# Prompt's pointwise jobs put ahead of four output units, partial sums added in DRAM, and the sample's last scaling spread out on GpSimd's queue

## The chip, the core and the metric

The kernel runs on one core of a Trainium2 chip. The metric is device microseconds of one execution, from the host's side; lower is better. TensorE (PE) does the matmuls, VectorE (DVE), ScalarE (ACT) and GpSimd (POOL) the rest, and SyncE (SP) issues most of the transfers between DRAM and SBUF. GpSimd issues the transfers that add into their target. In the listings of this text, `out<-in` names what an instruction writes and reads, and a number behind a name is a buffer's.

## What is computed

One encoder layer over two sequences with shared weights: the *sample* (1024 positions) and the *prompt* (512), both with 2048 channels in fp32.

```python
def mixer_layer(x, norm_g, w_in, w_dw, b_dw, ln_g, ln_b, w_pw, sink, w_out):
    h = rms_norm(x, norm_g)
    z = h @ w_in                       # conv value, glu, gate; q, k, v; attention gate
    ...
    conv_out = conformer_conv(c_val, c_glu, w_dw, b_dw, ln_g, ln_b, w_pw) * silu(c_gate)
    attn_out = banded_sink_attention(q, k, v, sink) * silu(a_gate)
    mix = concatenate([conv_out, attn_out], axis=-1) @ w_out
    return x + mix

y = rms_norm(mixer_layer(x, ...), final_norm_g)     # for x_prompt and x_sample
```

Inside `conformer_conv` a layer norm and a silu stand ahead of the *pointwise* product with `w_pw` (1024 x 1024). The case here lies in the last steps of both sequences: the prompt's pointwise product, its product with `w_out`, the sum with x and the last norm; and for the sample only the last norm's scaling.

## The kernel before

Every fp32 product is made of three matmuls on parts of reduced precision: a value is split into a high part (a copy on ACT, line 449) and a low part (a subtraction on DVE, line 450), and high x high, high x low and low x high are summed in a PSUM bank. On top of this the large products use a Strassen-like scheme: a *unit* takes a 2 x 2 arrangement of weight blocks and token blocks and forms seven products P1, P2, P6, P5, P7, P3, P4 of sums and differences of blocks. So weights need subtractions on DVE (line 138, `sub`) before they are split, and so do tokens.

The end of the program runs in this order. `over[1]` are eight units of the sample's out-projection, the last of which is called `end`; each finished piece goes to `y_d` in DRAM and its squares are summed (`Mix.project`). Then come four *wide* units for the prompt's out-projection (class `Wide`), each with p, the half of the output's columns, and g, the half of the input channels: g = 1 is the attention's half, g = 0 the convolution's. A wide unit has seven steps of 24 matmuls of 128x512 and loads fourteen tiles of 512 KB, eight of `w_last` (weights in rows) and six of `low_out` (low parts stored earlier by the sample's units). Between the second and the third wide unit stand the prompt's eight pointwise *jobs* `fj`, of 24 matmuls each, since the g = 0 units need their result as tokens.

The parts that the change touches:

- **The prompt's partial sums.** In a g = 1 unit, `Wide.tap` (line 1678) takes a finished bank out with ACT or DVE, adds banks of the same output block on DVE (line 1693, 1699) and stores four sums for each of two row blocks into `part_d` (called `rows` in listings), in pieces of 512 bytes. Before the g = 0 units, `load_rows` (line 1515) loads rows of x into SBUF by SP and then adds `part_d` to them by a transfer of GpSimd (line 429, `add_into`). In g = 0 units `add_rows` (line 1532) adds each bank to these rows on DVE (line 1536), and after the last one takes squares, multiplies by the gain, scales and stores.
- **The sample's last scaling.** `Mix.finish` (line 1280) waits until all squares are there, makes the factors, and then, for each of 16 channel blocks, loads 512 KB of `y_d`, multiplies on DVE (line 1311) and stores to `y_s`, all by SP. It is a generator on the lane `prep`, which advances by a credit of nanoseconds for each matmul group that is written out; `yield 2500` is the price of one block.
- **Buffers.** T1 (28 tiles of 4 KB per partition) holds tokens and wide weights, F (7), A (4), G (4) and U (4) hold rows and intermediate results. `E()` takes from G and U in turn. `raw` (3) and `hl` (3) hold weights ahead of and behind the split. A load into a buffer waits until the last reader of what was in it is done.

Engines run their instructions in the order of the listing. A scheduler that knows dependences and priorities makes that order from the program, so an instruction without dependences may be listed far ahead of where the code asks for it. A wait holds up all that stands behind it on the same engine or queue.

Of the kernel before, what the change touches and what calls it, by code (L numbers as in the profile page):

```python
# [7 lines left out]
F32 = mybir.dt.float32  # L8
# [1144 lines left out]
class Mix:  # L1153


    def __init__(self, e, seq, out):
# [8 lines left out]
        self.squared = 0  # L1165
        self.beside = []
# [113 lines left out]
    def finish(self):  # L1280
# [28 lines left out]
        for o in range(ND):  # L1309
            y = held.popleft()  # L1310
            nc.vector.scalar_tensor_tensor(y, y, e.fin_g[:, o : o + 1], rb, ALU.mult, ALU.mult)
            e.store(self.out[o], y)
            y = None
            load(o + 2)
            yield 2500
# [126 lines left out]
class LastPost(Post):  # L1442


    def __init__(self, e, seq, t0, out, mix):
# [3 lines left out]
        self.x, self.s1 = [], {}  # L1449
        self.part_d = [[e.tc.dram_tile([P, NB, 2, P], F32, name=f"rows_{b}{c}") for c in range(2)] for b in range(NB)]  # L1450
# [15 lines left out]
    def load_attention(self):  # L1466
        e = self.e
        for h in range(0, HEADS, 2):
            t = (e.F if h < HALF else e.A)([2, W], F32)
            e.nc.sync.dma_start(t, self.seq.att_d[h // GROUP][:, h % GROUP : h % GROUP + 2, :])  # L1470
            self.x.append(t)

    def load_gate(self, i):
# [3 lines left out]
        if i % 2 == 0:  # L1477
            t = e.A([2, W], F32)
            self.x.append(t)
# [4 lines left out]
    def mixed(self, i, f):  # L1484
        if i % 2:
            n = i // 2 % 2
            self.token(0, "A11" if i < HALF else "A12", n)
            if i == HALF + 1:
                self.token(0, "S2", n)

    def token(self, g, name, n):
# [3 lines left out]
        x0 = half(self.x[n])  # L1495
        x1 = half(self.x[n + 2]) if name != "A11" else None
# [11 lines left out]
        if name == "A22" and n == 1:  # L1508
            self.x = []
# [4 lines left out]

    def load_rows(self, c, room):
        e, half = self.e, D // 2
        for b in range(NB):
            t = self.rows[b][c] = room([half], F32)
            e.nc.sync.dma_start(t, self.e.a["x_p"][b * P : (b + 1) * P, c * half : (c + 1) * half])
        for b in range(NB):  # L1520
            e.add_into(self.rows[b][c], self.part_d[b][c].rearrange("p a c x -> p (a c x)"))

    def load_gain(self):
        e, half = self.e, D // 2
        for c in range(2):
            self.gain[c] = e.F([half])
# [36 lines left out]
class Wide(Unit):  # L1563


    def __init__(self, e, last, p, g, tags):
# [4 lines left out]
        self.raw, self.low, self.sum, self.d = {}, {}, {}, {}  # L1571
# [107 lines left out]
    def tap(self, name, q):  # L1679

        e, nc, d = self.e, self.e.nc, self.d
# [9 lines left out]
        if name in ("P2", "P3"):  # L1691
            x = d.pop((q, c))
            nc.vector.tensor_tensor(x, bank, x, ALU.add)
        else:
            x = e.PT("p", NP, [W]) if name == "P6" else e.E()
            nc.scalar.activation(x, bank, AF.Copy)
            if name == "P7":
                y = d.pop((q, 2))
                nc.vector.tensor_tensor(x, x, y, ALU.add)
            elif name != "P4":  # L1700
                d[q, {"P1": 0, "P6": 1, "P5": 2}[name]] = x
        if last:
            e.store_later(self.last.part_d[b][self.p][:, :, c, :], x.rearrange("p (a x) -> p a x", a=NB))


def encoder(ctx, tc, a):
# [234 lines left out]
    def norm_last():  # L1941
# [9 lines left out]
        Wide(e, last, 0, 1, ("ss", "bc", "aa")),  # L1951
        Wide(e, last, 1, 1, (("pt", "pv"), "bc", "aa")),
        Wide(e, last, 0, 0, (("pt", "pv"), "bc", "aa")),
        Wide(e, last, 1, 0, ("ss", "bc", "aa")),
# [8 lines left out]
    end.before.append(last.load_attention)  # L1963
    for step, name in enumerate(names):
        at(end, step, lambda name=name: e.T.pop(name))
    for unit, step, name in ((end, 0, 0), (end, 2, 1), (end, 4, 2), (wide[0], 0, 3), (wide[0], 1, 4), (wide[0], 2, 5), (wide[0], 3, 6)):
        at(unit, step, lambda name=names[name]: last.tokens(1, name))
    for step, name in enumerate(names):
        at(wide[1], step, lambda name=name: last.tok[1].pop(name))
        at(wide[3], step, lambda name=name: last.tok[0].pop(name))  # L1970
    wide[1].before.append(lambda: e.prep.add(mix.finish()))
    pace(wide[1], 1.5, e.prep)
    for step in (2, 4):
        for i in range(4):
# [67 lines left out]
```

## Time and profile before

| | us |
|---|---|
| three runs, median (lowest to highest) | 2160.98 (2159.86 to 2161.76) |
| the profiled execution | 2158.56 |
| its span in the trace | 2156.8 |
| TensorE busy | 2072.4 (96% of the span) |
| DVE, ACT, POOL busy | 1750.3, 1133.6, 111.8 |
| bytes moved by DMA | 498.72 MB, mean 231 GB/s |

The span is the trace's own length, from the first to the last instruction; the 1.8 us between it and the execution's time lie around it. "L1311" is line 1311 of the program. A row of waits names who waited for what. TensorE's busy time counts modelled ends of pipelined matmuls, so the idle time is better read from stretches than from the sum. SP's and POOL's transfers run on queues that the profile calls q1 (SP) and q0 (POOL).

### The profile page before, as it was taken

The page shows a single profiled execution, that of the slowest core. Times are in us where ns is not written, and L with a number is a line of the kernel's source. Part 1 is how long each engine was busy: PE and PEld are TensorE (multiplying, and loading weights), DVE is VectorE, ACT ScalarE, POOL GpSimd, SP SyncE. Part 2 cuts the span into 40 slices and gives each one's busy share as a digit, 9 for nine tenths or more (in the row PEclk, how much of TensorE's full clock was granted, in tenths as well). Part 3 has the DMA queues.
Part 4 walks back from the last instruction along what each step waited for, and adds up shares of the span by engine and source line. Part 5 has one row for each costly group of instructions (what it writes and reads, how often), then busy time and mean ns, then how long its engine had stood idle before and what let it go on. Part 6 is the DMA issues. An engine that isn't in the chain of part 4 may idle for free.

```text
span 2156.8 us, 26835 instructions
## 1 busy us (share of the span) xinstructions
PE 2072.4 (96%) x9234; PEld 1695.2 (79%) x9234; DVE 1750.3 (81%) x2655; ACT 1133.6 (53%) x1832; POOL 111.8 (5%) x132
## 2 busy tenths in 40 slices
PE   8999999999999999999999999999999999979857
PEld 7878888888888887788888888878878888758646
DVE  8657798988898988988987786578997779687747
ACT  7475445333555556555556764245644645555324
POOL 0001110000011111000000000000000011100000
PEclk9999999999999999999999999999999999989979
DMA  8888888854777778654465548977896699987884
GB/s 298 291 287 242 227 185 265 284 175 144 245 180 181 167 161 268 209 176 152 150 211 181 183 135 293 324 251 260 283 301 215 198 296 267 281 298 250 337 248 152
DMA packets 246713, 498.72 MB, mean 231 GB/s; under 512 B 22704, under 2 KB 84528, under 8 KB 246576
## 3 DMA queue, kind: packets, MB, share of 16 engines
q1 hardware_dynamic: 227136, 458.72, 63.3%
q0 software_dynamic: 18432, 35.66, 10.2%
q10 hardware_dynamic: 1008, 2.63, 0.3%
q8 instruction: 72, 1.18, 0.2%
q14 instruction: 65, 0.53, 0.1%
HBM read 335.97 MB, written 160.96 MB: 230 GB/s over the span
## 4 chain that ended last, share of the span: by engine, by line
PE 79%; DMA 10%; DVE 5%; issue 3%; ACT 2%; POOL 0%; SPq 0%; POOLq 0%; ACTq 0%; DVEq 0%
PE a L191 23%; PE a L588 12%; PE c L191 11%; PE c L588 6%; PE b L191 6%; PE b L588 5%; PE s L191 3%; PE s L1052 2%; PE pv L1084 2%; PE a L1641 2%; PE s L1641 2%; DVE hl L450 1%; DMA f<-x_s 1%; PE pt L1089 1%; DMA f<-rows 1%
## 5 line engine op out<-in xcount | busy, mean ns | idle before, releaser
L191 PE MATMUL a<-t,hl 128*128 128x512 f32 x2640 | 633.4, 390 | 6.7 <-ACT u L217 4.2
L191 PEld LDWEIGHTS a<-t,hl 128*128 128x128 f32 x2640 | 493.5, 188 | 113.3 <-ACT u L217 6.7
L925 DVE SCALAR_TENSOR_TENSOR f<-f,c_w_dw,f 128x1024 f32<-128x1024 f32 (+1 forms) x464 | 455.9, 1015 | 0.9 <-ACT f L920 0.8
L450 DVE TENSOR_TENSOR hl<-raw,hl 128x1024 fp32r<-128x1024 f32 (+1 forms) x304 | 306.8, 1009 | 155.9 <-ACT hl L449 154.9
L449 ACT ACTIVATE hl<-raw 128x1024 fp32r<-128x1024 f32 (+1 forms) x304 | 268.9, 885 | 300.6 <-DVE raw L138 59.4
L588 PE MATMUL a<-t,hl 128*128 128x512 f32 x1344 | 328.5, 394 | 1.1 <-DVE hl L450 1.1
L191 PE MATMUL c<-t,hl 128*128 128x512 f32 x1320 | 319.5, 390 | 1.7 <-ACT u L217 0.9
L191 PEld LDWEIGHTS c<-t,hl 128*128 128x128 f32 x1320 | 247.5, 188 | 54.6 <-ACT g L217 1.7
L588 PEld LDWEIGHTS a<-t,hl 128*128 128x128 f32 x1344 | 248.6, 188 | 52.2 <-DVE hl L450 2.2
L588 PE MATMUL c<-t,hl 128*128 128x512 f32 x672 | 166.1, 394 | 0.9 <-DVE hl L450 0.6
L588 PE MATMUL b<-t,hl 128*128 128x512 f32 x672 | 164.0, 393 | 0.7 <-DVE hl L450 0.7
L191 PE MATMUL b<-t,hl 128*128 128x512 f32 x660 | 161.6, 390 | 0.0
L588 PEld LDWEIGHTS b<-t,hl 128*128 128x128 f32 x672 | 124.6, 188 | 26.1 <-DVE hl L450 1.1
L588 PEld LDWEIGHTS c<-t,hl 128*128 128x128 f32 x672 | 124.1, 188 | 26.0 <-DVE hl L450 1.0
L191 PEld LDWEIGHTS b<-t,hl 128*128 128x128 f32 x660 | 123.4, 188 | 25.2
L217 ACT ACTIVATE u<-a 128x512 f32<-128x512 f32 x114 | 67.4, 592 | 86.5 <-PE a L191 64.6
L217 ACT ACTIVATE g<-a 128x512 f32<-128x512 f32 x106 | 62.8, 592 | 76.2 <-PE a L191 68.2
L1641 PE MATMUL a<-hl,t 128*128 128x512 f32 x160 | 50.4, 439 | 28.4 <-DVE f L1536 14.2
L1066 ACT ACTIVATE p<-p,tiny 128x384 f32<-128x384 f32 (+1 forms) x96 | 54.5, 570 | 30.1 <-DVE tiny L1063 18.8
L449 ACT ACTIVATE a<-pt 128x512 fp32r<-128x512 f32 x64 | 38.0, 594 | 51.9 <-PE pt L1089 51.7
L346 ACT ACTIVATE hl<-raw 128x1024 fp32r<-128x1024 f32 x44 | 46.3, 1052 | 35.6 <-PE a L588 12.4
L1641 PEld LDWEIGHTS a<-hl,t 128*128 128x128 f32 x160 | 33.2, 212 | 39.2 <-issue 14.3
(354 smaller groups left out, 2690.7 us busy)
## 6 DMA issues: line engine op xcount, KB each, us to landing
raw<-w_in SPq DMA_DIRECT2D x171, 512.0 KB, 4.8
t<-w_last SPq DMA_DIRECT2D x32, 512.0 KB, 7.8
raw<-w_out SPq DMA_DIRECT2D x31, 512.0 KB, 5.4
a<-xT_s SPq DMA_DIRECT2D x50, 256.0 KB, 5.4
raw<-w_pw SPq DMA_DIRECT2D x24, 512.0 KB, 5.1
t<-low_out SPq DMA_DIRECT2D x24, 512.0 KB, 8.1
f<-x_s SPq DMA_DIRECT2D x16, 512.0 KB, 7.2
low_out<-hl SPq DMA_DIRECT2D x16, 512.0 KB, 4.2
```

The lines of the kernel that those rows point to most:

```text
L191: nc.tensor.matmul(acc, hl[:, l, o, j, :], toks[j][:, r], start=name in FRESH and j == 0 and q == 0, stop=name in LAST and j == HALF - 1 a ...
L217: nc.scalar.activation(t, bank, AF.Copy)
L346: e.nc.scalar.activation(t[:, 0], raw, AF.Copy)
L449: nc.scalar.activation(hi, x, AF.Copy)
L450: nc.vector.tensor_tensor(lo, x, hi.bitcast(F32), ALU.subtract)
L588: nc.tensor.matmul(job.acc[0], hl[:, l, kk // HALF, kk % HALF, :], r, start=i == 0 and p == 0, stop=i == nk - 1 and p == 2,)
L925: nc.vector.scalar_tensor_tensor(t, h[:, j : j + T], w(j), t, ALU.mult, ALU.add)
L1052: nc.tensor.matmul(ps[:, 0:n], qs[:, x, h], k[y][:, keys], start=p == 0, stop=p == 2)
L1066: nc.scalar.activation(p[:, 0:n], p[:, 0:n], AF.Exp, bias=nm[:, h : h + 1], accum_out=l[:, h : h + 1])
L1084: nc.tensor.matmul(pv, v[x][:, vs], pt[:, y], start=i == 0 and p == 0, stop=i == last and p == 2)
L1089: nc.tensor.transpose(tp[:, h], p[:, i * P : (i + 1) * P], e.ident)
L1641: nc.tensor.matmul(self.bank[n][q], tok[h][:, r, i, q * P : (q + 1) * P], e.hl[at[h]][l][:, i], start=name in FRESH and j == 0 and p == 0, ...
```

## The change

The eight pointwise jobs now stand ahead of all four wide units. The sums of the g = 1 units are no longer formed in SBUF: x is copied to `part_d` ahead of time, each bank is copied out by ACT and added into `part_d` by a transfer of GpSimd, and the rows are then loaded whole. The sample's scaling takes a price of 8000 in place of 2500 for each block, and its loads and stores go in halves through GpSimd's queue. The gain is loaded into raw buffers in place of F buffers. The prompt's tokens are made by `tokens` alone, in steps of the wide units, and the units' PSUM banks are dealt anew.

```diff
 # Mix.finish
-                nc.sync.dma_start(held[-1], self.y_d[o])
+                for t in (0, W):
+                    nc.gpsimd.dma_start(held[-1][:, t : t + W], self.y_d[o][:, t : t + W])
...
+        self.spread = True
...
-            e.store(self.out[o], y)
+            for t in (0, W):
+                nc.gpsimd.dma_start(self.out[o][:, t : t + W], y[:, t : t + W])
             y = None
             load(o + 2)
-            yield 2500
+            yield 8000
 # LastPost
-        self.part_d = [[e.tc.dram_tile([P, NB, 2, P], F32, ...
+        self.part_d = [[e.tc.dram_tile([P, 2, W], F32, ...
...
+    def copy_row(self, b, c):
+        e, half = self.e, D // 2
+        src = e.a["x_p"][b * P : (b + 1) * P, c * half : (c + 1) * half]
+        for i in range(2):
+            dst = self.part_d[b][c][:, i].rearrange("p (a x) -> p a x", a=NB)
+            e.nc.sync.dma_start(dst, src.rearrange("p (a c x) -> p a c x", a=NB, c=2)[:, :, i])

     def load_rows(self, c, room):
         for b in range(NB):
             t = self.rows[b][c] = room([half], F32)
-            e.nc.sync.dma_start(t, self.e.a["x_p"][b * P : (b + 1) * P, c * half : (c + 1) * half])
-        for b in range(NB):
-            e.add_into(self.rows[b][c], self.part_d[b][c].rearrange("p a c x -> p (a c x)"))
+            for i in range(2):
+                e.nc.sync.dma_start(self.columns(t, i), self.part_d[b][c][:, i].rearrange("p (a x) -> p a x", a=NB))

     def load_gain(self):
-            self.gain[c] = e.F([half])
+            self.gain[c] = e.raw_tile().rearrange("p a b c -> p (a b c)")
 # Wide.tap, g == 1
-        if name in ("P2", "P3"):
-            x = d.pop((q, c))
-            nc.vector.tensor_tensor(x, bank, x, ALU.add)
-        else:
-            x = e.PT("p", NP, [W]) if name == "P6" else e.E()
-            nc.scalar.activation(x, bank, AF.Copy)
...
-        if last:
-            e.store_later(self.last.part_d[b][self.p][:, :, c, :], x.rearrange("p (a x) -> p a x", a=NB))
+        x = e.E()
+        nc.scalar.activation(x, bank, AF.Copy)
+        e.add_into(self.last.part_d[b][self.p][:, c], x)
 # encoder
+    for n, unit in enumerate(over[1]):
+        at(unit, 3, lambda n=n: last.copy_row(n // 2, n % 2))
...
-    fj[3].before.append(lambda: last.load_rows(0, e.F))
-    fj[7].before.append(last.load_gain)
...
+    fj[1].before.append(lambda: e.prep.add(mix.finish()))
+    pace(fj[1], 1.5, e.prep)
...
+    wide[1].before.append(lambda: until(lambda: mix.spread, e.prep))
+    at(wide[1], 2, last.load_gain)
+    at(wide[1], 4, lambda: last.load_rows(0, e.F))
+    at(wide[2], 3, lambda: last.load_rows(1, e.A))
+    at(wide[3], 3, e.prep.drain)
...
-    jobs += [[wide[0]], [wide[1]]] + [[j] for j in fj] + [[wide[2]], [wide[3]]]
+    jobs += [[j] for j in fj] + [[w] for w in wide]
```

Three places in the listings show what moves. The first is SP's queue ahead of the third wide unit, before the change: the loads of x (L1519) stand behind the stores of the sample's rows and between the unit's weights, and GpSimd's adds wait for them.

```order
L432 DMA y_s<-f_2541_17003 128x1024
L432 DMA y_s<-f_2542_17013 128x1024
L432 DMA y_s<-f_2547_17035 128x1024
L1519 DMA f_2550_17068<-x_p 128x1024
L1519 DMA f_2551_17070<-x_p 128x1024
L1593 DMA t1_2619_17473<-w_last 128x1024
L1598 DMA t1_2620_17475<-low_out_10_414 128x1024
```

After the change the same queue, at the end of the pointwise jobs' loads: the last job's weights, two loads of the gain, and then the loads of the first wide unit.

```order
L332 DMA raw_2420_16404<-w_pw 128x1024
L1485 DMA a_2438_16505<-gate_d1_7_168 128x512
L1532 DMA raw_2551_17114<-final_gain 128x1024
L1532 DMA raw_2552_17116<-final_gain 128x1024
L1598 DMA t1_2445_16529<-w_last 128x1024
L1603 DMA t1_2446_16531<-low_out_00_412 128x1024
L1598 DMA t1_2449_16561<-w_last 128x1024
L1603 DMA t1_2450_16563<-low_out_00_412 128x1024
```

The sample's rows and x are gone from here; the weights follow one another. The second place is the wide units. GpSimd's queue after the change, from the first step of the first wide unit on: `rows` are the adds of banks (L429), `y_s` and `y_d` the sample's stores and loads (L1316, L1289).

```order
L429 DMA rows_10_266<-g_2472_16666 128x512
L1316 DMA y_s<-f_2463_16620 128x512 x2
L429 DMA rows_00_264<-u_2480_16717 128x512
L429 DMA rows_10_266<-g_2481_16720 128x512
L1289 DMA f_2466_16646<-y_d_2_206 128x512 x2
L429 DMA rows_00_264<-u_2491_16775 128x512
L429 DMA rows_10_266<-g_2492_16778 128x512
L1316 DMA y_s<-f_2464_16623 128x512 x2
L1289 DMA f_2477_16702<-y_d_3_207 128x512 x2
```

Before, this queue held eight adds into rows behind the last out-projection unit's and nothing else; now adds, stores and loads take turns in it. DVE in the second wide unit after the change: L1314 is the sample's scaling, L450 a low part of weights (`hl`) or tokens (`t1`).

```order
L450 TENSOR_TENSOR hl_2557_17129<-t1_2519_16931,hl_2557_17129 128x1024
L1314 SCALAR_TENSOR_TENSOR f_2531_17007<-f_2531_17007,c_final_norm_g_957,f_2220_15033 128x1024
L450 TENSOR_TENSOR hl_2559_17151<-t1_2522_16949,hl_2559_17151 128x1024
L450 TENSOR_TENSOR t1_2561_17168<-a_2391_16219,t1_2561_17168 128x512
L450 TENSOR_TENSOR t1_2563_17175<-a_2399_16291,t1_2563_17175 128x512
L1314 SCALAR_TENSOR_TENSOR f_2546_17078<-f_2546_17078,c_final_norm_g_957,f_2220_15033 128x1024
```

Before, most of these scalings stood among the pointwise jobs, and four of them in a row ahead of the third unit's tokens. The third place is SP's queue near the program's start, as one piece of the difference: the copies of x to `rows` (L1519), which the code asks for in `over[1]`, are listed among the first stage's stores and loads.

```order
 L432 DMA part_conv_01_293<-u_909 128x512
+L1519 DMA rows_264<-x_p 128x4x128
 L432 DMA part_conv_10_288<-g_1011 128x512
+L1519 DMA rows_264<-x_p 128x4x128
+L1519 DMA rows_265<-x_p 128x4x128
 L432 DMA part_conv_10_294<-u_1038 128x512
+L1519 DMA rows_265<-x_p 128x4x128
+L1519 DMA rows_266<-x_p 128x4x128
 L123 DMA raw_1044<-w_in 128x1024
```

Six of the sixteen copies stand here; the other ten follow within a hundred rows.

More of the change, by code (lines that the diff above doesn't have):

```diff
@@ L1448, in __init__ @@
         self.tok = {0: {}, 1: {}}
[L1449 to L1450 removed]
+        self.x, self.s1 = {0: [], 1: []}, {}
+        self.part_d = [[e.tc.dram_tile([P, 2, W], F32, name=f"rows_{b}{c}") for c in range(2)] for b in range(NB)]
         self.rows = [[None, None] for _ in range(NB)]
@@ L1570, in __init__ @@
         self.order = ALONE
-        self.raw, self.low, self.sum, self.d = {}, {}, {}, {}
+        self.raw, self.low, self.sum = {}, {}, {}
     LOADS = {"P1": [(0, 0)], "P2": [(0, 1)], "P6": [(1, 0), (1, 1)]}
@@ L1950, in encoder @@
     wide = [
[L1951 to L1954, printed above, removed]
+        Wide(e, last, p, g, banks)
+        for p, g, banks in (
+            (0, 1, (("pt", "pv"), "bc", "aa")),
+            (1, 1, ("ss", "bc", "aa")),
+            (0, 0, (("pt", "pv"), "bc", "aa")),
+            (1, 0, ("ss", "bc", "aa")),
+        )
     ]
@@ L1962, in encoder @@
     end = over[1][-1]
-    end.before.append(last.load_attention)
     for step, name in enumerate(names):
         at(end, step, lambda name=name: e.T.pop(name))
-    for unit, step, name in ((end, 0, 0), (end, 2, 1), (end, 4, 2), (wide[0], 0, 3), (wide[0], 1, 4), (wide[0], 2, 5), (wide[0], 3, 6)):
-        at(unit, step, lambda name=names[name]: last.tokens(1, name))
-    for step, name in enumerate(names):
         at(wide[1], step, lambda name=name: last.tok[1].pop(name))
         at(wide[3], step, lambda name=name: last.tok[0].pop(name))
[L1971 to L1974, printed above, removed]
-            at(wide[1], step, lambda i=i, step=step: last.split(2 * step - 4 + i))
+    for step in range(2):
+        for i in range(4 * step, 4 * step + 4):
+            at(end, step, lambda i=i: last.split(i))
+    at(end, 2, last.load_attention)
+    for n, unit in enumerate(over[1]):
+        at(unit, 3, lambda n=n: last.copy_row(n // 2, n % 2))
     def run_out():
@@ L1979, in run_out @@
             e.turn_over(True)
-    fj[3].before.append(run_out)
-    fj[3].before.append(lambda: last.load_rows(0, e.F))
-    fj[7].before.append(e.prep.drain)
-    fj[7].before.append(last.load_gain)
-    for step, name in ((0, 2), (0, 3), (1, 4), (2, 5), (3, 6)):
-        at(wide[2], step, lambda name=names[name]: last.tokens(0, name))
-    at(wide[2], 0, last.cs.clear)
-    at(wide[2], 4, lambda: last.load_rows(1, e.A))
-    jobs += [[wide[0]], [wide[1]]] + [[j] for j in fj] + [[wide[2]], [wide[3]]]
+    fj[5].before.append(run_out)
+    fj[1].before.append(lambda: e.prep.add(mix.finish()))
+    pace(fj[1], 1.5, e.prep)
+    for n, name in ((2, 0), (4, 1), (6, 2)):
+        fj[n].before.append(lambda name=names[name]: last.tokens(1, name))
+    for step, name in enumerate(names[3:]):
+        at(wide[0], step, lambda name=name: last.tokens(1, name))
+    at(wide[0], 0, last.cs.clear)
+    for step, name in enumerate(names):
+        unit, n = (wide[1], step + 1) if step < 5 else (wide[2], step - 5)
+        at(unit, n, lambda name=name: last.tokens(0, name))
+    wide[1].before.append(lambda: until(lambda: mix.spread, e.prep))
[4 more added lines that the diff above has]
+    jobs += [[j] for j in fj] + [[w] for w in wide]
     e.weights_setup(jobs)
```

25 lines of the change are left out of this document (8 added, 17 removed).

## The prediction

> **What bounds the kernel now.** I first cut the end of the run into its stages with the view that sums busy time by stretch. The columns are the stretch and its length, then the busy time of PE, PEld, DVE, ACT and POOL, the granted TensorE clock (1.00 is full), the mean busy share of the 16 DMA engines, and GB/s.
>
> ```profile
> 1700.00:1883.00 183.00, 180.55 (x797) 147.02 (x796) 146.13 (x226) 106.74 (x178) 27.03 (x31) 1.00 0.94 276
> 1883.00:1941.00 58.00, 44.25 (x168) 33.88 (x167) 45.25 (x57) 29.19 (x41) 0.86 (x1) 0.85 0.88 298
> 1941.00:1982.00 41.00, 41.00 (x190) 33.95 (x189) 33.08 (x65) 26.78 (x37) 0.00 (x0) 1.00 0.67 217
> 1982.00:2026.00 44.00, 44.00 (x196) 36.45 (x195) 28.64 (x31) 11.77 (x14) 0.00 (x0) 1.00 0.97 353
> 2026.00:2105.00 79.00, 46.52 (x169) 34.72 (x168) 46.90 (x56) 24.16 (x36) 4.56 (x6) 0.78 0.82 269
> 2105.00:2143.50 38.50, 38.50 (x171) 31.64 (x169) 33.11 (x58) 19.87 (x32) 2.40 (x3) 1.00 0.34 85
> 2143.50:2156.80 13.30, 0.12 (x1) 0.00 (x0) 6.08 (x22) 4.46 (x9) 0.00 (x0) 0.68 0.80 316
> ```
>
> The rows are: the last out-projection units, the first wide unit, the second, the eight pointwise jobs, the third wide unit, the fourth, the tail. TensorE is full in all but the first and third wide units. All four units have the same matmuls, and the fourth shows what one costs when it is served: 38.5 us. The second takes 41.0 with extra small matmuls for the sample's norm. So the four parts between 1883 and 2105 need 44.0 + 41.0 + 2 x 38.5 = 162 us of TensorE and take 222: **60 us are lost**, 19.5 in the first unit and 40.5 in the third, part of it to a clock that is not granted in full (0.85 and 0.78). This is all that the end of the kernel can give. Next, the waits, first TensorE's own from 1883 to 2106, then the longest of DVE in 2026 to 2106 (total, times, longest).
>
> ```profile
> PE a L1641 <- DVE f L1536: 14.2, 2, 13.9
> PE a L1641 <- DVE t L450: 9.4, 2, 7.1
> PE s L1641 <- ACT hl L449: 8.5, 1, 8.5
> PE pt L1641 <- DVE f L1536: 6.4, 2, 5.6
> ...
> DVE f L1536 <- DMA f<-rows: 22.5, 4, 10.7
> ```
>
> In the third unit TensorE waits for a free bank, the bank for DVE's add into the rows (L1536), and DVE for the rows, which came by two transfers in series (x, then an accumulating one). In the first unit the waits (ACT hl L449, DVE t L450) are for weights and tokens that are late. Last, the queues and issues from 1883 to 2105 (packets, MB, share of 16 engines; KB each, us to landing).
>
> ```profile
> q1 hardware_dynamic: 24900, 59.40, 75.3%
> q0 software_dynamic: 1152, 3.41, 8.3%
> ...
> t<-w_last SPq DMA_DIRECT2D x28, 512.0 KB, 7.5
> t<-low_out SPq DMA_DIRECT2D x19, 512.0 KB, 7.6
> f<-y_d SPq DMA_DIRECT2D x16, 512.0 KB, 6.5
> y_s<-f SPq DMA_DIRECT2D x16, 512.0 KB, 6.3
> ...
> f<-x_p SPq DMA_DIRECT2D x4, 512.0 KB, 6.1
> f<-rows POOLq DMA_DIRECT2D x4, 512.0 KB, 11.1
> a<-x_p SPq DMA_DIRECT2D x4, 512.0 KB, 7.2
> rows<-g SPq DMA_DIRECT2D x6, 256.0 KB, 3.8
> rows<-u SPq DMA_DIRECT2D x6, 256.0 KB, 3.8
> rows<-p SPq DMA_DIRECT2D x4, 256.0 KB, 3.1
> ```
>
> So beside TensorE stands a second resource that is nearly full: 83.6% of 222 us, 186 us of all 16 engines. TensorE needs 162 us, the transfers 186. The 60 us are waits in series today, but 24 us of them remain even if every wait goes, unless bytes go or move.
>
> **The change part by part.** *Order of stages.* The pointwise jobs come directly behind the out-projection. They need weights through the raw buffers, and eight split tiles made in the last out-projection unit, so the first unit's late weights no longer face an idle TensorE: the listing has one unit's loads issued under the jobs. Two gain loads stand ahead of twelve of these on SP's queue and wait for raw buffers, until about the fourth job (22 us in); 22 us are left for 14 x 0.52 = 7.3 MB, which at the 353 GB/s of the jobs' row take 21. I cost this at nothing; without that cover it would be a few us at the first unit's start. The splits (8 on ACT, 8 on DVE) move into a stretch where DVE is busy 146 of 183 us and ACT 107, so they fit.
>
> *Rows.* The third unit's serial wait (x_p, then 11.1 us) goes, since the loads are issued in the second unit. What is late next is the DMA engines. Prices: on q1, 0.753 x 222 = 167 us for 59.40 MB, 2.81 us per MB. An accumulating transfer, from the window, 0.083 x 222 / 3.41 = 5.4 us per MB; over the whole run:
>
> ```profile
> q0 software_dynamic: 18432, 35.66, 10.2%
> ```
>
> 0.102 x 2156.8 / 35.66 = 6.2, twice the price of a plain one (191 ns of an engine per packet against 96 if q1's price is put on the same 2 KB). Plain bytes of the same stretch afterwards: 59.4, less x_p (8 x 0.52 = 4.2), less the stores to rows (16 x 0.26 = 4.2), plus 16 row loads of 0.26 (4.2): **55.2 MB, 155 us**. Accumulating: 14 adds per unit and two units, 28 x 0.26 = 7.3 MB, and one old one: 7.6 MB at 5.4 to 6.2, **44 us**. Together **199 us**, where there were 186. The work on DVE shrinks by 12 adds and ACT's grows by 8 copies of some 0.6 us, both beside TensorE.
>
> The change thus takes away waits and adds 13 us to the resource that is nearly full. If the engines run unbroken, the stretch takes 199 us instead of 222: TensorE loses 37 instead of 60, **a gain of 23 us**. The place is the second and third unit's weights and the sample's rows. The fourth unit and the tail (38.5 and 13.3) stay.
>
> The bounds of the prices. The best stretch of the page's kind:
>
> ```profile
> 2020.00:2040.00 20.00, 17.18 (x76) 13.89 (x74) 16.60 (x20) 9.14 (x12) 0.00 (x0) 1.00 1.01 405
> ```
>
> At 405 GB/s a MB costs 2.5 us: 55.2 MB take 138, with the adds at 5.4 (41) 179, lost 17, gain 43. If the engines hold only the 0.94 of the first row above, 199 / 0.94 = 212, lost 50, gain 10. No run shows an add whose target is DRAM; the rows above have SBUF as target. Below, it could cost as little as a plain one (2.8 us per MB: 23 us less); less than plain is excluded, since it moves the same bytes. Above, I allow twice the seen price (12.4 at most: some 45 us more). I take the seen price, the nearest row.
>
> The Trainium skill, "DMA: Bandwidth & Descriptors", section on issuing engines that are not separate DMA queues, says that transfers issued by GpSimd, SP or ACT run on the same 16 engines, and that another issuer saves only issue time. It speaks against the move of the sample's 16.8 MB to GpSimd's queue; by it the sum is the 199 us above. Were it wrong, SP's queue would keep 38.4 MB, 108 us, below TensorE's 162, and nearly all 60 us would come back. No row before the change tries it, but no stretch here shows a share much over 1.
>
> *The sample's scaling.* Per row it is one DVE operation:
>
> ```profile
> L1311 DVE SCALAR_TENSOR_TENSOR f<-f,c_final_norm_g,f 128x1024 f32<-128x1024 f32 x16 | 20.0, 1279 | 2.0 <-DMA f<-y_d 2.0
> ...
> L429 POOL DMA_DIRECT2D g<-part_out x16 | 14.5, 907 | 67.0 <-DVE g L237 39.8 <-ACT g L217 11.3 <-DMA f<-att_d 7.4
> ```
>
> The listing has sixteen such operations strewn from the first unit's start to the third's middle, one every 6 us. Halves make 64 issues on POOL beside 28 adds: 92 x 0.9 = 83 us of POOL in 162, which fits. What is new is the wait: behind each scaling on DVE stand the next low parts of weights and tokens, and the row it waits for is issued on POOL behind adds that wait for ACT's copies, and behind the store that frees its buffer.
>
> *Copies of x.* The code asks for them in the out-projection; the listing puts all 16 (4.2 MB, 12 us at 2.81) among the first loads.
>
> ```profile
> 40.00:170.00 130.00, 126.79 (x553) 102.85 (x552) 86.98 (x144) 80.50 (x134) 0.00 (x0) 1.00 0.87 295
> ```
>
> There 13% of 130 us, 17 us, are free, so most is hidden; bounds 0 and 12 us, and I take **2 us**.
>
> **Sum.** The profiled execution took 2158.56 us, 2.4 below the median of the runs shown. 2158.6 - 23 + 2 = 2137.6; on the median's scale **2140**.
>
> **The rivals.** *Hidden after all:* adds in DRAM cost what plain transfers do, or the engines run at the best stretch's rate. Gain 35 to 60, so 2103 to 2128. For it: rates of 405 exist. Against it: mixed stretches run at 250 to 350.
>
> *GpSimd's queue in series:* while only two buffers turn over, a row needs a store (two issues of 0.9, landing 6.3), a load (1.8 and 6.5) and the scaling (1.3): 17.7 us for two rows, 8.8 each, against 5.5 us for a step of TensorE (38.5 / 7). Some five rows are held so, 5 x 3.3 = 17 us if that time doesn't fall on the engines' own excess: 2157. For it: the listing's order. Against: four more buffers come free in the first unit.
>
> *Slower, by the price of an add in DRAM:* 28 adds are 224 packets of 2 KB on each engine, so each ns more per packet adds 0.224 us. The net gain of 21 us is gone when a packet costs 94 ns more than 191, from about **285 ns**; at twice the price, 382 ns, the result is 2161 - 21 + 43 = 2183. For it: the sum already exceeds TensorE's work, so every added us shows. Against: adds from DRAM into SBUF cost just two plain packets.
>
> **How the numbers follow.** The forecast (gain 10 to 34, 2129 to 2153) has 0.45, the hidden case 0.18, the queue in series 0.17 (2150 to 2160, about 0.05 of it clear of no change), the dear adds 0.20 (2163 to 2185). The forecast's own range is 2129 to 2153; for 8 in 10 it must reach into both outer cases: 2112 to 2172. About 0.2%, 4.3 us, is what a measurement of this kernel can tell from no change. Faster 0.45 + 0.18 + 0.05 = 0.68, within 0.12, slower 0.20.
>
> **What would show it.** Right: behind the out-projection the jobs run full; DVE no longer waits for rows; the three wide units after them take about 155 us at a DMA share of 0.95 or more; TensorE waits there for low parts of weights that stand behind the scaling on DVE. q0 carries some 56 MB (35.7, less 4.2 for the rows' old adds, plus 7.3 and 16.8), and its adds cost near 191 ns per packet. The first 170 us stay as full as they are. Wrong: a DMA share well under 0.9 in the wide units with TensorE waiting (series on a queue), TensorE full there (hidden), or a long row of waits for ACT's copies to find a free buffer (dear adds).

## The result, and the profile after

| | before | after |
|---|---|---|
| median of 4 runs (lowest to highest), us | 2161.02 (2159.86 to 2161.76) | 2146.86 (2142.96 to 2149.76) |
| the profiled execution, its span | 2158.56, 2156.8 | 2147.58, 2145.8 |

The ratio is 0.9934, interval 0.9917 to 0.9951: faster by 14.2 us, where 21 were forecast, inside the range. First the view that sums busy time by stretch, cut at the ends of the stages after the change: the eight pointwise jobs, the four wide units, the tail. The columns are those of the prediction's first view.

```profile
1888.60:1934.50 45.90, 45.90 (x212) 38.21 (x211) 26.96 (x62) 14.39 (x19) 1.75 (x2) 1.00 0.89 319
1934.50:1989.60 55.10, 43.20 (x170) 33.47 (x169) 36.75 (x41) 27.73 (x39) 21.16 (x31) 0.88 0.91 267
1989.60:2040.20 50.60, 43.37 (x170) 34.10 (x169) 35.26 (x38) 28.35 (x41) 22.73 (x36) 0.90 1.04 332
2040.20:2094.10 53.90, 40.70 (x170) 32.62 (x169) 35.52 (x42) 19.79 (x30) 14.07 (x22) 0.87 1.01 318
2094.10:2132.00 37.90, 37.90 (x168) 31.00 (x167) 34.58 (x60) 19.23 (x33) 0.00 (x0) 1.00 0.14 44
2132.00:2145.80 13.80, 1.06 (x5) 0.56 (x3) 6.87 (x24) 5.39 (x9) 0.00 (x0) 0.69 0.77 304
```

The jobs are full, and so is the fourth unit (37.9). The first three units, at 55.1, 50.6 and 53.9, lose 45.9 us against it, where the stretch of before lost 60. The DMA engines stand at 0.91 to 1.04 in them, and at 0.14 in the fourth. From the jobs' start to the third unit's end it takes 205.3 us, before 221.8. The queues in just that stretch (packets, MB, share of 16 engines):

```profile
q1 hardware_dynamic: 17894, 38.67, 52.1%
q0 software_dynamic: 9440, 24.40, 44.0%
```

That is 96.1% of 205.3 us, or 197 us of all engines, where 199 were forecast. So the transfers cost what was worked out; the stretch is longer than they are. What TensorE waits for from 1875 us on (total, times, longest):

```profile
PE a L1646 <- DVE hl L450: 11.8, 1, 11.8
PE pt L1646 <- DVE hl L450: 8.5, 2, 7.6
PE s L1646 <- DVE hl L450: 7.2, 3, 4.3
PE pt L1646 <- ACT hl L449: 2.7, 1, 2.7
```

And DVE, in the wide units:

```profile
DVE f L1314 <- DMA f<-y_d: 50.7, 8, 11.6
```

The old waits for the prompt's rows (DVE f L1536, 22.5 us) are gone. In their place 27.5 of 32.4 us of TensorE's waits are for low parts of weights (`hl`, L450), and DVE, which makes them, stands 50.7 us ahead of the sample's scaling (L1314) until its row has come. The rest of the 45.9 us is clock. In the timeline of TensorE's matmuls (start, us, what, how many, idle before):

```profile
1974.88 0.50 PE L1646 MATMUL pt<-hl,t 128*128 128x512 f32 x1 [0.91 <-DVE t L450]
1982.94 0.79 PE L1646 MATMUL pt<-hl,t 128*128 128x512 f32 x1 [7.56 <-DVE hl L450]
1983.53 1.48 PE L1646 MATMUL pv<-hl,t 128*128 128x512 f32 x3
1984.81 1.48 PE L1646 MATMUL pt<-hl,t 128*128 128x512 f32 x3
...
1987.96 0.85 PE L1646 MATMUL pv<-hl,t 128*128 128x512 f32 x3
1988.65 0.85 PE L1646 MATMUL pt<-hl,t 128*128 128x512 f32 x3
```

Behind a wait of 7.56 us three matmuls take 1.28 us from one start to the next (1983.53 to 1984.81), and some 4 us later 0.69 (1987.96 to 1988.65). So a wait costs more than its own length: 32.4 us of waits, and some 13 more at a granted clock of 0.87 to 0.90. The Trainium skill, "TensorE: Matmul & The Clock Gate", Part 1, says that the clock falls to half after an idle window of about 3.4 us and comes back after as long a busy one; these rows agree, with slow matmuls for some 4 us behind a wait of 7.56.

### The profile page after: what moved, and what is told of

Read it like the earlier page. It is cut to its first block, busy times and chain, and to the rows that moved or that the text cites. A ratio compares the mean times of both kernels' runs of the same rounds, so it can differ in the third digit from the quotient of the medians.

```text
span 2145.8 us, 26961 instructions
## 1 busy us (share of the span) xinstructions
PE 2073.5 (97%) x9234; PEld 1698.2 (79%) x9234; DVE 1740.5 (81%) x2643; ACT 1136.5 (53%) x1840; POOL 165.2 (8%) x216
## 3 DMA queue, kind: packets, MB, share of 16 engines
q0 software_dynamic: 26432, 55.59, 13.2%
## 4 chain that ended last, share of the span: by engine, by line
PE 76%; DMA 9%; DVE 7%; issue 4%; ACT 2%; POOL 1%; SPq 1%; ACTq 0%; POOLq 0%; DVEq 0%
PE a L191 23%; PE a L588 12%; PE c L191 11%; PE b L588 6%; PE c L588 6%; PE b L191 6%; PE s L1052 2%; PE pv L1084 2%; DMA f<-y_d 2%; PE s L191 2%; DVE hl L450 2%; PE pt L1089 1%; PE s L1646 1%; DMA f<-x_s 1%; DVE f L925 1%
## 5 line engine op out<-in xcount | busy, mean ns | idle before, releaser
L450 DVE TENSOR_TENSOR hl<-raw,hl 128x1024 fp32r<-128x1024 f32 (+1 forms) x304 | 305.7, 1005 | 156.6 <-ACT hl L449 155.5
L588 PEld LDWEIGHTS b<-t,hl 128*128 128x128 f32 x672 | 124.5, 188 | 26.1 <-DVE hl L450 1.1
L429 POOL DMA_DIRECT2D u<-part_out x16 | 14.0, 893 | 933.4 <-DMA f<-msum_S 875.7
L1066 ACT ACTIVATE p<-p,tiny 128x384 f32<-128x384 f32 (+1 forms) x96 | 54.5, 570 | 32.3 <-DVE tiny L1063 21.1
L449 ACT ACTIVATE t<-f 128x512 fp32r<-128x512 f32 x87 | 50.4, 622 | 31.8 <-DMA f<-cs 13.3
L449 ACT ACTIVATE a<-pt 128x512 fp32r<-128x512 f32 x64 | 38.0, 593 | 52.2 <-PE pt L1089 52.0
```

What stands on the lines that cost most here:

```text
L449: nc.scalar.activation(hi, x, AF.Copy)
L450: nc.vector.tensor_tensor(lo, x, hi.bitcast(F32), ALU.subtract)
L588: nc.tensor.matmul(job.acc[0], hl[:, l, kk // HALF, kk % HALF, :], r, start=i == 0 and p == 0, stop=i == nk - 1 and p == 2,)
L1066: nc.scalar.activation(p[:, 0:n], p[:, 0:n], AF.Exp, bias=nm[:, h : h + 1], accum_out=l[:, h : h + 1])
```

## The experiments

Two theories were set against each other. *A, engine time:* the prediction's, that the transfers' time on the 16 engines sets the length of the wide units. *B, order:* the sample's rows are late because their loads and stores take turns with the adds in GpSimd's queue, and DVE waits for them ahead of the low parts. Each ratio is to the kernel before, timed beside the run. The lengths of the four units are worked out from the start times of the matmuls in the profiled execution (168 per unit, from the back; the last column is their sum), good to about half a microsecond. `price14000` and `no_finish` leave out part of the sample's scaling, and `plain_stores` the sums.

| run | median, us | ratio to before (interval) | wide units 1, 2, 3, 4 | sum |
|---|---|---|---|---|
| the change | 2146.9 | 0.9934 (0.9917 to 0.9951) | 55.1, 50.6, 53.9, 38.2 | 197.8 |
| `after_again` | 2146.9 | 0.9937 (0.9922 to 0.9951) | 54.9, 51.3, 52.6, 38.1 | 196.9 |
| `plain_stores` | 2124.9 | 0.9839 (0.9823 to 0.9855) | 51.8, 38.1, 50.8, 37.9 | 178.6 |
| `sp_finish` | 2146.7 | 0.9936 (0.9920 to 0.9953) | 44.1, 50.7, 63.4, 37.8 | 196.0 |
| `price14000` | 2135.2 | 0.9885 (0.9871 to 0.9900) | 44.2, 40.9, 59.2, 40.0 | 184.3 |
| `price13000` | 2137.0 | 0.9905 (0.9883 to 0.9927) | 44.1, 42.9, 60.5, 37.9 | 185.4 |
| `sbuf_sums` | 2141.4 | 0.9925 (0.9906 to 0.9945) | 54.5, 41.0, 58.7, 40.5 | 194.7 |
| `sums_spread11` | 2137.4 | 0.9909 (0.9888 to 0.9931) | 46.2, 41.7, 55.8, 40.9 | 184.6 |
| `order_only` | 2148.0 | 0.9933 (0.9918 to 0.9948) | 48.2, 57.7, 54.4, 37.9 | 198.2 |
| `rows_late` | 2146.2 | 0.9924 (0.9909 to 0.9939) | 54.4, 51.0, 53.4, 38.1 | 196.9 |
| `rows_sums_spread` | 2138.3 | 0.9889 (0.9873 to 0.9906) | 46.9, 40.1, 59.0, 40.5 | 186.5 |
| `no_finish` | 2119.2 | 0.9808 (0.9788 to 0.9827) | 44.1, 38.7, 52.2, 37.9 | 172.9 |

**The adds as plain stores.**

```diff
-        e.add_into(self.last.part_d[b][self.p][:, c], x)
+        nc.gpsimd.dma_start(self.last.part_d[b][self.p][:, c], x)
```

> The 28 adds of prompt's banks in DRAM are replaced by plain transfers of the same bytes, issued from the same places of GpSimd's queue (the sums with x and between banks are left out). Theory A, the DMA engines' time bounds the three wide units: 7.3 MB times (6.2 - 2.8) us per MB = 25 us of engine time go, and the end stretch shrinks by 15 to 25 us against the changed kernel (time 2122 to 2132). Theory B, order: the sample's rows come late because their loads and stores take turns with adds in GpSimd's queue, and DVE waits for them ahead of the weights' low parts; the order stays, so under 5 us are won (2142 to 2147) and DVE's wait for rows of y_d stays near 50 us.

22 us less on the medians, as A had it; B is out with its 5 (the units' sum falls by 19, in an execution that took 2129.7). Over the same 159.4 us (1934.5 to 2093.9) GpSimd's queue carries the same bytes in both. First the change, then this run:

```profile
q0 software_dynamic: 8832, 23.07, 53.1%
```

```profile
q0 software_dynamic: 7040, 23.07, 37.5%
```

The difference, 15.6% of 159.4, is 24.9 us of engine time for 7.34 MB of adds, 3.4 us per MB above a plain transfer: the forecast's 6.2 - 2.8, at its upper price. The run doesn't part the engines' time from all of B, though: DVE's wait for the sample's rows, which B had staying near 50 us, falls as well, to

```profile
DVE f L1314 <- DMA f<-y_d: 21.0, 6, 6.6
```

**The sample's rows on SP's queue.**

```diff
-                for t in (0, W):
-                    nc.gpsimd.dma_start(held[-1][:, t : t + W], self.y_d[o][:, t : t + W])
+                nc.sync.dma_start(held[-1], self.y_d[o])
...
-            for t in (0, W):
-                nc.gpsimd.dma_start(self.out[o][:, t : t + W], y[:, t : t + W])
+            e.store(self.out[o], y)
```

> The sample's loads and stores go through SP's queue again, 512 KB each, at the same price of 8000 per block; all else is the changed kernel. Theory A (DMA engines' time): the bytes stay, so within 3 us of the changed kernel (2144 to 2150). Theory B (order in GpSimd's queue): DVE's wait for rows of y_d, 50.7 us in the changed kernel, changes by half or more, and the time by over 5 us with it, downwards if SP serves the rows sooner, upwards if they then stand behind weights that wait for buffers.

The time is the same to 0.2 us, as A had it. Of B, the change of the wait came, and not that of the time: DVE's wait for these rows falls from 50.7 to

```profile
DVE f L1313 <- DMA f<-y_d: 15.2, 8, 7.5
```

and yet only the place of the loss moves. The first unit takes 44.1 in place of 55.1, the third 63.4 in place of 53.9, and the sum is 196.0 against 197.8. That fits A: a wait that is taken away and comes back elsewhere, with the sum kept, looks like a symptom. But two effects of order that cancel aren't ruled out by this run. SP itself now stands ahead of the third unit's weights, at stores of the sample's rows that wait for DVE's scaling (SP, 1990 to 2045):

```profile
SPq L432 <- DVE f L1313: 20.6, 5, 11.0
```

Here q0 carries the adds alone, which gives their price by itself:

```profile
q0 software_dynamic: 4032, 7.34, 25.7%
```

0.257 x 159.4 / 7.34 = 5.6 us per MB, in the forecast's 5.4 to 6.2. The Trainium skill, "DMA: Bandwidth & Descriptors", section on issuing engines that are not separate DMA queues, says that transfers run on the same 16 engines whoever issues them, and that another issuer saves only the time of issuing; the run agrees in its time, 2146.7 against 2146.9.

**The scaling spread into the fourth unit.** Two runs, since in the first the drain stood where it is never reached, so that it leaves the last two blocks out.

```diff
-            yield 8000
+            yield 14000
...
-    at(wide[3], 3, e.prep.drain)
+    at(wide[3], 6, e.prep.drain)
```

> The sample's scaling gets a price of 14000 per block in place of 8000, and its drain stands at step 6 of the fourth unit in place of step 3, so that by the listing some five of the sixteen blocks move from the first three units into the fourth, where the DMA engines were 6% busy. Theory A (DMA engines' time): 5 x 1.05 MB x 2.8 us = 15 us of transfers leave the full stretch; the time falls by 8 to 15 us (2132 to 2139), with nothing lost in the fourth unit. Theory B (order): the same number of scalings less stand ahead of low parts, so the wait falls in proportion, 5 of 16, some 10 us at the most; it doesn't tell the two apart, but if the time falls by under 4 us both are wrong about what the sample's rows cost.

The second has `yield 13000` and the drain at step 5, and scales all blocks.

> The changed kernel with a price of 13000 per block and the drain at step 5 of the fourth unit, so that all sixteen blocks are scaled (the run with 14000 left the last two of sixteen blocks out, since a drain at step 6 of that unit is never reached). About 4 blocks move into the fourth unit, 4 x 1.05 x 2.6 = 11 us of transfers: 2134 to 2140 by theory A. If the last blocks' loads and stores come behind the fourth unit's end, the tail grows beyond 13.8 us and takes some of it back.

Both came inside A's range, the first with two blocks of work less. The stage rows of the second show what is won and what isn't (units 1 to 4, then the tail):

```profile
1928.80:1972.90 44.10, 40.65 (x169) 32.27 (x168) 38.60 (x45) 26.94 (x38) 13.89 (x20) 0.96 0.86 252
1972.90:2015.80 42.90, 40.04 (x170) 32.64 (x169) 31.43 (x34) 26.59 (x37) 20.71 (x29) 0.96 1.03 277
2015.80:2076.30 60.50, 42.42 (x169) 32.43 (x168) 35.08 (x40) 22.12 (x34) 14.05 (x22) 0.89 1.06 357
2076.30:2114.20 37.90, 37.90 (x168) 31.37 (x168) 35.91 (x54) 18.62 (x30) 8.31 (x16) 1.00 0.36 125
2114.20:2132.40 18.20, 3.11 (x14) 2.25 (x12) 10.62 (x35) 6.82 (x14) 1.08 (x2) 0.73 0.74 291
```

The fourth unit takes the moved blocks at no cost (DMA share 0.36 for 0.14, still 37.9 us), the first two units come nearer to full, and the tail grows from 13.8 to 18.2 us, as expected. But the third unit is longer than in the change, 60.5 for 53.9. What TensorE and DVE wait for in it, and the timeline of DVE around that:

```profile
PE pt L1646 <- DVE f L1541: 13.0, 1, 13.0
```

```profile
DVE t L138 <- DMA t<-w_last: 24.8, 4, 23.0
```

```profile
2035.63 1.22 DVE L138 TENSOR_TENSOR t<-t,t 128x1024 f32<-128x1024 f32 x1 [23.04 <-DMA t<-w_last]
2036.78 0.68 DVE L450 TENSOR_TENSOR t<-a,t 128x512 fp32r<-128x512 f32 x1
2038.21 2.36 DVE L138 TENSOR_TENSOR t<-t,t 128x1024 f32<-128x1024 f32 x2 [0.75 <-DMA t<-w_last]
```

DVE's next instruction is a subtraction of weights for the third step (L138), and its tile of `w_last` comes 23 us late. Behind it in DVE's order stands the first add of a bank into the rows (L1541), and TensorE needs that bank. One reason why the tile is late stands in SP's waits, from 1985 to 2030:

```profile
SPq L1526 <- DMA y_s<-f: 34.4, 4, 22.2
```

The loads of prompt's rows (L1526) wait for F tiles until the sample's rows in them are stored, 22.2 us for one, and the third unit's weights stand behind them on SP. In SP's timeline two of these rows go out at 2006.96 and the first of the weights at 2008.01, 8 us ahead of their unit. The other reason is the engines. Asked for so late, the weights meet the rest of the traffic: the DMA share is 1.06 in this unit, and in 2007 to 2036 a tile of `w_last` takes 19.1 us to land, where the change takes 9.7 in 2000 to 2040 at the same share:

```profile
t<-w_last SPq DMA_DIRECT2D x8, 512.0 KB, 19.1
```

The two aren't parted by this run.

**The sums in SBUF again.** The old `tap` (lines 1689 to 1701 of the kernel before), with its finished sums added into the copied x: 16 adds in DRAM in place of 28.

```diff
-        x = e.E()
-        nc.scalar.activation(x, bank, AF.Copy)
-        e.add_into(self.last.part_d[b][self.p][:, c], x)
+        if name in ("P2", "P3"):
+            x = d.pop((q, c))
+            nc.vector.tensor_tensor(x, bank, x, ALU.add)
+        else:
+            ...
+        if last:
+            e.add_into(self.last.part_d[b][self.p][:, c], x)
```

> The sums of the g = 1 units are formed in SBUF again as in the kernel before (DVE adds banks, four sums per row block), and only the finished sums are added into the copied x: 16 adds in DRAM in place of 28; all else is the changed kernel. Theory A (DMA engines' time): 12 adds of 0.262 MB at 5.6 us per MB (the adds' price in the run with the sample's rows on SP's queue) are 17.6 us of engine time less, so the time falls by 11 to 18 us against 2146.9 (2129 to 2136). Rival C, DVE and buffers: 12 additions of DVE and sums that hold buffers for up to four steps come back, and the time falls by less than 6 us (2141 or more), with DVE's or ACT's waits for these buffers in the first two units.

A miss: 2141.4, 5.5 us less (by the ratios 0.9925 and 0.9937 under 3), not 11 to 18. The transfers did shrink, since in 1886 to 2090 they hold

```profile
q1 hardware_dynamic: 17047, 38.99, 53.6%
q0 software_dynamic: 7405, 20.24, 35.5%
```

89.1% of 204 us, 182 for the change's 197. The second unit falls by 9.6 us to 41.0, but the third rises by 4.8 and the fourth by 2.3, and the first stays at 54.5. C's row, a wait of DVE or ACT for buffers of sums, isn't among the longest waits there; the row of SP is, in 1985 to 2035:

```profile
SPq L1526 <- DMA y_s<-f: 23.4, 3, 13.8
```

In the changed kernel it is 2.0 us in all. So engine time summed over the stretch doesn't set the length alone: some of what is freed is lost again in the third unit. The rows that hold SP are the likely reason, though SP also waits there 13.1 us for a tile that TensorE reads (L1603 <- PE s).

**Three more.** `sums_spread11` joins the SBUF sums, a price of 11000 and the drain at step 5.

> Sums in SBUF (16 adds) together with a price of 11000 per block for the sample's scaling and its drain at step 5 of the fourth unit. By theory A the engine time of the full stretch falls by 17.6 us and by some 3 blocks more, 3 x 1.05 MB x 2.6 = 8 us: the first three units then have about 170 us of transfers beside 162 of TensorE, so 2118 to 2128, under which nothing is left in the stretch but TensorE's own work. If it stays above 2132, another wait takes over, and it is named by its row.

A miss again: 2137.4, no better than the price alone. The third unit stays at 55.8, with the same row at 33.4 us (one wait of 20.6). `order_only` has the new order of stages, the copied x and the rows loaded whole, but sums in SBUF and the scaling on SP at 2500, as before.

> The new order of stages, the copied x and the rows loaded whole, but the sums in SBUF and the sample's scaling as in the kernel before: 512 KB loads and stores on SP's queue at a price of 2500. Against the run with sums in SBUF alone (2141.4) only the pace and the queue of the scaling are undone. Theory A: the same bytes, in the same full stretch but pushed forward by some blocks: 2141 to 2148, so nearly the whole gain comes from the order and the rows. If the spread over time is worth much, as the fall to 2137 with prices of 11000 to 13000 lets one think, nearer to 2150.

2148.0, ratio 0.9933. That is the change's own gain. So the order, the rows and what else stays in this run (the gain's buffers, the tokens, the banks) bring all of it, and the 28 adds together with the spread at 8000 on GpSimd's queue bring nothing. One by one they may do more: by the medians the spread brings 6.6 us (2148.0 to 2141.4 of `sbuf_sums`) and the twelve adds more take 5.5 back, but by the ratios (0.9933, 0.9925, 0.9934) neither is clear of the noise. Order and rows weren't tried apart. `rows_late` loads the second half of the rows later:

```diff
-    def load_rows(self, c, room):
+    def load_rows(self, c, room, rows=range(NB)):
...
-    at(wide[2], 3, lambda: last.load_rows(1, e.A))
+    at(wide[2], 6, lambda: last.load_rows(1, e.A, (0, 1)))
+    at(wide[3], 1, lambda: last.load_rows(1, e.A, (2, 3)))
```

> The changed kernel, but the second half of prompt's rows (8 loads of 0.262 MB in pieces of 512 bytes, used only in the fourth unit) is loaded at step 6 of the third unit and step 1 of the fourth, not at step 3 of the third. Theory A (DMA engines' time in the full stretch): no byte goes, but up to 2.1 MB x 3.3 us per MB = 7 us of engine time leave the full stretch for the fourth unit, where the engines are 14% busy: 3 to 7 us off 2146.9 (2140 to 2144). If the third unit's end hangs on something else (a weight that a buffer holds back), no change (2145 to 2149); if the fourth unit then waits for its rows, slower.

No change, but it says nothing on A, since the loads hardly moved. The row of line 1526 (count, issue ns, first and last start), first of the change, then of this run:

```profile
L1526 SPq DMA_DIRECT2D a<-rows x8: 371/486/3409, 2072.4 to 2090.8; - x8
```

```profile
L1526 SPq DMA_DIRECT2D a<-rows x8: 371/494/3022, 2070.6 to 2088.9; - x8
```

The listing placed them there in either case. The same edit on top of `sums_spread11` moved the sum of the units from 184.6 to 186.5:

> Three edits in one: sums in SBUF (16 adds in DRAM), a price of 11000 per block of the sample's scaling with the drain at step 5 of the fourth unit, and the second half of prompt's rows loaded late. Without the last edit it took 2137.4, and its third unit 55.8 us where 38.1 is full, at a DMA share of 1.05 for its first 40 us. Theory A: 3 to 7 us less, 2130 to 2135. If it stays within 2 us of 2137, the rows' loads weren't what the third unit's weights waited behind.

By the ratios the two are one (0.9889 and 0.9909). By the expectation, the rows' loads weren't then what the third unit's weights waited behind. But the edit moves the second half of the rows only, and hardly moves it (first and last start 2033.6 and 2087.7, against 2033.5 and 2086.4); the first half, which holds SP, stayed where it was. So the run says nothing on that half.

**Without the sample's scaling.** Only the first two of sixteen blocks are loaded, scaled and stored.

```diff
-        for o in range(ND):
+        for o in range(2):
...
-            load(o + 2)
+            pass
```

> The changed kernel without 14 of the 16 blocks of the sample's last scaling: their loads, multiplications and stores are left out, so most of the sample's output isn't written. That takes 14.7 MB and, at 2.6 us per MB, 38 us of DMA engine time out of the wide units, and nearly all of DVE's waits for the sample's rows. The four units lost 45 us of TensorE in the changed kernel. Theory A (DMA engines' time): 45 falls to 10 or less, since 197 us of transfers become some 159 beside 162 of TensorE: 2108 to 2118. Rival D (buffers: each unit's first eight to twelve loads are wanted within its first three steps, and tiles for them come free only as the unit before is used up): 20 us or more of the loss stay, 2122 or more, with the DMA engines idle ahead of each unit's start.

2119.2 lies between the two. The four units take 172.9 us; against four of 37.9 they lose 21 where the change loses 46, so 25 of the 46 us go with 38 us of transfers and with DVE's waits for them, and 21 stay. Units 1 to 4:

```profile
1931.60:1975.70 44.10, 40.66 (x170) 32.41 (x169) 33.38 (x37) 28.04 (x40) 11.95 (x15) 0.96 0.85 249
1975.70:2014.40 38.70, 38.45 (x170) 31.38 (x169) 25.90 (x30) 28.03 (x41) 12.24 (x14) 1.00 1.07 276
2014.40:2066.60 52.20, 40.42 (x170) 32.55 (x169) 35.18 (x41) 19.78 (x30) 2.62 (x3) 0.87 0.80 250
2066.60:2104.50 37.90, 37.72 (x167) 30.91 (x165) 32.13 (x58) 19.70 (x33) 0.00 (x0) 1.00 0.08 28
```

The loss stands in the first unit (6) and above all in the third (14). Its one long wait there is the one of the run with 13000, and SP's row is there too, now with the adds in DRAM as what the rows wait for (TensorE in 2014 to 2067; SP in 1975 to 2030):

```profile
PE pt L1646 <- DVE f L1541: 11.3, 1, 11.3
```

```profile
SPq L1526 <- DMA rows<-u: 22.8, 4, 9.7
```

Over the whole third unit the DMA share is 0.80, but the mean hides the time that counts. Up to 2022, just ahead of TensorE's wait (2024 to 2036), the engines are full, and the weights asked for in 2000 to 2015 take 18.6 us to land:

```profile
2001.00:2022.00 21.00, 21.00 (x95) 17.38 (x94) 4.43 (x5) 12.54 (x18) 6.13 (x7) 1.00 1.08 313
2022.00:2036.00 14.00, 2.86 (x13) 2.04 (x11) 9.82 (x11) 3.06 (x3) 0.88 (x1) 0.68 0.83 244
```

```profile
t<-w_last SPq DMA_DIRECT2D x4, 512.0 KB, 18.6
```

In the first unit it is again a load of rows that holds SP, for 26.1 us (SP in 1912 to 1956), while the DMA share is 0.51 from 1931.6 to 1946:

```profile
SPq L1526 <- DMA y_s<-f: 26.7, 2, 26.1
```

So at the most 25 of the 46 us speak for A, and D, as it was put, isn't shown in this run. Tiles that matmuls still read hold SP's loads in the changed kernel, between 1918 and 1956:

```profile
SPq L1603 <- PE a L588: 10.7, 2, 10.4
SPq L1598 <- PE c L1646: 9.8, 1, 9.8
```

For the 14 us of the third unit the rows suggest a third mechanism: loads of rows that wait, on the queue that carries the weights, so that the weights are asked for late and all at once. It is read from the rows of five traces (`price13000`, `sbuf_sums`, `sums_spread11`, `rows_sums_spread`, `no_finish`) and not shown. It isn't the only way to a long third unit: `sp_finish` has the longest (63.4) and `order_only` 54.4, and there these loads wait little or not at all. A run that takes these loads from SP's queue wasn't made.

**The front.** `after_again` is the change, `before_again` the kernel before, once more.

> The changed kernel once more, with nothing edited. In its first profile the 28 adds and 32 sample transfers made the end stretch (from the first pointwise job to the end of the last wide unit) 16 us shorter than before, but the program reached this stretch 5.7 us later than before, because of two stalls near 1330 and 1420 us, in code that the change does not touch. If these stalls are chance: time between 2141 and 2150 again, the lag of TensorE behind the kernel before, matmul for matmul, another one than 5.7 us at the start of the end stretch (0 to 6), and the end stretch again 16 us shorter, give or take 3. If the early copies or new code cause them: 5 to 6 us of lag at the same matmuls again.

> The kernel before once more, for its scatter ahead of the end stretch. Against the first profile of before, the changed kernel and its variants reach the end stretch 2.4 to 7.0 us late, with stalls at different places in each. If this is chance, the kernel before shows a lag of the same kind (1 to 6 us) in a second profile, and a time nearer to 2161. If the change causes it, the second profile lies within 1 us of the first at every matmul up to there.

The kernel before took 2158.2 us in its one further run. All traces have the same 9234 matmuls, and up to the 8300th in nearly the same order, so the start of the n-th, counted from the trace's first matmul and less the same in the first profile of before, is the lag. At the 1000th (some 235 us, behind the copies of x) the change and the eleven traces of its variants lag by -0.2 to 2.7 us, 1.2 in the mean, and `before_again` by 2.4. At the 8300th they lag by 0.0 to 7.0, 4.1 in the mean (the change 5.7, `after_again` 5.8), and `before_again` by 2.6. The copies cost nothing that these traces can tell. Later, a granted clock of half stands near 885 us in ten of the twelve traces and near 1430 us in nine, in neither of the two of before; the lag grows by 0.8 us around the first (3000th to 4000th matmul, in the mean) and 2.0 around the second (5900th to 6600th), that of `before_again` by -0.2 and 0.4. So 1 to 3 us of the change's time seem to be lost far ahead of what it touches. By what, wasn't tried, and two profiles of before are few.

## Why the prediction was right, and where its size was off

*Direction, range and mechanism held.* The time lies in the forecast's own range, 2129 to 2153. The waits in series for rows went, the jobs and the fourth unit ran full, TensorE waits for low parts that stand behind the scaling on DVE, and the DMA engines are full in two of the three units and in most of the other. q0 carried 55.59 MB (some 56 were expected), an add cost 5.6 us per MB (5.4 to 6.2), the transfers of the stretch took 197 us (199). The gain loads, costed at nothing, held SP until 1914, and the first unit still ran full until 1945: their cover sufficed. The copies, put at 2 us, show no cost. (Of them five, not six, stand in the piece of SP's queue that is printed with the change. The 96 ns per plain packet of 2 KB come out at 92 by the prediction's own 2.81 us per MB; nothing hangs on it.)

*The rivals fell.* Not hidden: 46 us are still lost. Not GpSimd's queue in series at its 2157: with the rows on SP's queue the time is the same, though another wait has come in place of the first. Not dear adds: the turning point was 285 ns per packet, and in `sp_finish` a packet of theirs took 163 ns of an engine (0.257 x 159.4 us x 16 / 4032), under the 191 that was taken; at 5.6 us per MB they cost about twice a plain transfer.

*The step that failed in size:* "If the engines run unbroken, the stretch takes 199 us instead of 222." The 199 us of work was right, the unbroken running was not; the stretch took 205.3, so 16.5 us were won and not 23. The break lies at the start of the first unit. This row and the next of the change show it:

```profile
1927.00:1955.00 28.00, 25.33 (x103) 19.75 (x102) 22.89 (x28) 13.97 (x20) 5.81 (x8) 0.94 0.68 195
1955.00:2070.00 115.00, 88.80 (x356) 70.27 (x354) 70.73 (x76) 54.32 (x76) 47.81 (x72) 0.88 1.04 324
```

In the 28 us before 1955 the engines are idle for a third, 9 us: SP has nothing that it may ask for until weight tiles come free (the two rows of 1918 to 1956 above), and the sample's first scaling runs at 1941.88 only. From 1955 on they are full for 115 us. So the sum of engine time was a floor here, and what the engines stood idle at this stage's start came on top of it. The other part of the gap between the profiled executions is the later start of the stretch: 5.4 us (1883.2 to 1888.6) where 2 were put. By parts: 6.5 (16.5 for 23) + 3.4 + 0.5 (tail 13.8 for 13.3) - 0.4 (fourth unit) = 10.0 us, which is 2147.6 less the 2137.6 of the sum. On the medians 6.9 are left of it, 2146.9 for 2140.

*What the prediction didn't see:* the gain comes without the spread at 8000 and with 16 adds in place of 28 (`order_only`), so those two together neither won nor lost; and the row loads, which the prediction followed only as bytes, are also waits on SP's queue ahead of the third unit's weights. That these decide the third unit's length in the faster versions is likely and not shown.

Three versions beat both kernels and scale all blocks: `price13000`, `sums_spread11` and `rows_sums_spread`, at 0.9905, 0.9909 and 0.9889. Their intervals overlap, so no order among them is claimed, and of the three only the last lies wholly below the change's (0.9917 to 0.9951); each puts transfers of the sample under the fourth unit.

## What to carry to other kernels

Sum the transfers' time on all engines where they are nearly as busy as the bounding engine (84% of the stretch here, before the change); take that sum as a floor, and look for what lies between it and the time at the starts of stages, where buffers, and loads that wait on the same queue ahead of others, bound what is asked for. When a wait is removed and the sum of the stages stays, look for the wait that has come in its place before calling the first a symptom; here moving bytes to a stretch where the engines idle won time, and changing the queue didn't. An add in flight cost about twice a plain transfer here (5.6 us per MB for 2.8).

## What was not expected of the hardware

An issue on SP can itself take long: of the loads of rows (line 1526) in the change half take under 0.48 us and one takes 7.7, while the DMA engines are full (1.06 in 2026 to 2034).

```profile
L1526 SPq DMA_DIRECT2D f<-rows x8: 359/479/7656, 2025.8 to 2057.1; - x8
```

What stands behind it on the queue waits meanwhile: the long one starts at 2026.92, the next at 2034.63. But full engines alone don't make it long. In `no_finish` seven of the same eight loads go out between 1968 and 1988, at a share of 1.08, and the longest of the eight takes 0.64 us:

```profile
L1526 SPq DMA_DIRECT2D f<-rows x8: 359/368/640, 1946.6 to 1987.9; - x8
1968.00:1988.00 20.00, 20.00 (x90) 16.46 (x89) 15.08 (x16) 11.11 (x17) 6.95 (x8) 1.00 1.08 256
```

What makes the issue long stays open.
